# State-space decays kept by head in a hybrid decoder trunk: a scan and broadcast loads in place of matmuls, and the second decay product ahead of the retention

## The chip, the cores and the metric

The kernel runs on one core of a Trainium2 chip. The metric is the device time of one execution in microseconds (us). TensorE (PE) multiplies matrices, VectorE (DVE), ScalarE (ACT) and GpSimd (POOL) work on tiles in the on-chip memory, and SyncE (SP) issues the transfers (DMAs). Each engine has its own list of instructions and works through it in order; where an instruction needs something of another engine or of a DMA, its engine waits there, with all that stands behind it.

## What is computed

Two layers of a decoder trunk on 256 positions of width 1024, all in float32. A layer normalises its input, multiplies it by one wide matrix, feeds three token mixers (a state-space one, retention, and gated linear attention, "gla"), gates and merges their results, and ends with a gated MLP. The change concerns the state-space mixer, and the place of one step of gla. The reference, cut to these:

```python
SEQ, SSM_HEADS, SSM_GROUPS, SSM_STATE = 256, 8, 2, 64
...
def chunked_scalar_decay(q, k, v, log_a, chunk):
    """y_t = sum_{s<=t} (q_t . k_s) exp(sum_{j=s+1..t} log_a_j) v_s per head, chunkwise.
...
xbc = jax.nn.silu(causal_dwconv(xbc, ssm_conv_w, ssm_conv_b))
xs, bm, cm = jnp.split(xbc, [SSM_INNER, SSM_INNER + SSM_GROUPS * SSM_STATE], axis=-1)
...
dt = jax.nn.softplus(dt_raw.astype(jnp.float32) + ssm_dt_bias.astype(jnp.float32))
a = -jnp.exp(ssm_a_log.astype(jnp.float32))
y_ssm = chunked_scalar_decay(ch, bh, xs * dt[..., None].astype(xs.dtype), dt * a, CHUNK)
y_ssm = (y_ssm + ssm_d[:, None] * xs).reshape(bsz, seq, SSM_INNER)
...
alpha_logits = (g_lr @ gla_w_alpha2 + gla_b_alpha).astype(jnp.float32)
log_alpha = (jax.nn.log_sigmoid(alpha_logits) / GLA_GATE_NORMALIZER)
```

So each of the 8 heads has a row `dt` of 256 numbers and a running sum `cum` of `dt * a`, 256 numbers, and the mixer needs, for every pair of positions (s, t) with s <= t, the factor exp(cum_t - cum_s). "The second decay product" is `g_lr @ gla_w_alpha2`.

## The kernel before

**Weights.** All weights come as float32 and are split into a high and a low part, so that three fast matmuls replace one exact one. The unit is a piece of 128x1024 numbers (512 KB). SP loads it (`raw`, L176), ACT casts it to the high part (`whi`, L183), DVE subtracts to get the low part (`wlo`, L184), and PE uses both. Six `whi`, six `wlo` and four `raw` buffers hold pieces ahead of their use. PE's weight matmuls are L227 to L229 (256 columns), L274 to L276 (512 columns) and L1034 to L1036; they write PSUM tiles `mm`. A stream of them ("weight stream") runs through the whole program.

**The rest in between.** `layer` is a generator that yields after each small step of the weight stream. The mixers are generators as well (`ssm`, `ret`, `alpha`, `gla`); `spawn` puts one in a list, and it goes on when as many steps have passed as its last `yield` says. These waits are the table `W`. A scheduler then sets the final order on each engine from what the code says is needed. PE's small matmuls of the mixers write the four PSUM tiles `mx`; a fifth user of `mx` waits until the oldest is read.

**The state-space mixer before** (`ssm`). The projected `dt_raw` lies in `small`: 8 rows with the high part (partitions 0 to 7) and 8 with the low part (64 to 71), 256 positions each. PE multiplies it by a 0/1 matrix `pick` (L572), which adds the two and turns them to positions on partitions: 128x16 (two halves of 8 heads). On that shape come softplus (`log1p`: ACT L297, DVE L298, four times), the product with `a` (L585, tile `da`), and the running sum by three matmuls with a triangle and a matrix of ones (L594 to L596). PE turns the sums back (L609), ACT and DVE split them (L611, L612), and for each pair of heads two matmuls with a column of `pick_r` (L620) spread the rows over 128 partitions; ACT subtracts the partition's own sum (L624, L626), POOL masks (L629) and ACT takes the exponential (L631), which gives a tile `dec` of 128x768 for a pair. There are four pairs and two `dec` buffers, the `st` buffers of retention. Scores of each of the two groups (L637, L638) are multiplied in by DVE (L642), and `scan_out` (L558, 24 small matmuls for a pair) multiplies by the values, four times in a layer. POOL makes the values (L602) and the direct term (L604). L590 turns `xbc` to positions.

**Retention and the decay product before.** `ret` loads its decay tiles (`st`, L720, from `ret_decay`), multiplies in the scores (L729, masked by DVE at L735) and calls `scan_out`. `alpha` does the second decay product (L784: `small` by `wa`, which goes to an `mx` tile), softplus on 128x512, and a scan (L797). It is spawned after the projection `rg`, one projection behind `ret`.

Of the kernel before, what the change touches and what calls it, by code (L numbers as in the profile page):

```python
# [9 lines left out]
F32 = mybir.dt.float32  # L10
# [32 lines left out]
W = (4, 5, 4, 4, 1, 6, 5, 3, 5, 3, 3, 5, 1, 4, 4, 6, 2, 4, 5, 8)  # L43
# [13 lines left out]
for _n, _w in (("mix_g", 8), ("ffn_g", 8), ("conv_w", 24), ("conv_b", 6),  # L57
               ("ssm_g", 4), ("ret_g", 4), ("gla_g", 4), ("b_alpha", 2), ("fconv_w", 132), ("fconv_b", 44),
               ("dt_bias", 8), ("a_log", 8), ("ssm_d", 8)):
    PO[_n] = _at  # L60
    _at += _w
# [66 lines left out]
def hybrid_trunk(ctx: ExitStack, tc: tile.TileContext, xT_in, x_in, wall, par, wa2, cst, phase, dret, fin, gbias, out):  # L128
# [5 lines left out]
    tmp = ctx.enter_context(tc.tile_pool(name="tmp", bufs=4))  # L134
    sm = ctx.enter_context(tc.tile_pool(name="sm", bufs=2))
# [8 lines left out]
    tri = cs[:, CO_TRI:CO_TRI + P]  # L144

    pick_r = cpool.tile([40, 8], F32R, name="pick_r")

    pick = cpool.tile([P, 8], F32, name="pick")
# [143 lines left out]
    def log1p(e, q, p):  # L292

        n = e.shape[-1]
        for i, (_, m) in enumerate(LOG1P):
            qi = q[:, (i % 2) * n:(i % 2 + 1) * n]
            nc.scalar.activation(qi, e, AF.Square, scale=LOG1P_S, bias=lb[:, i:i + 1])  # L297
# [132 lines left out]
    class Mixers:  # L430
# [3 lines left out]
        def __init__(self, l, norm):  # L434
# [5 lines left out]
            self.aneg = sm.tile([P, 8], F32, name="aneg", tag="aneg")  # L440
            nc.scalar.activation(self.aneg, self.pc("a_log", 0, 8), AF.Exp)
# [125 lines left out]
        def ssm(self):  # L567
            xbc, rh, small = self.xbc, self.norm.rh, self.small
            yield W[0]
            pt = mx_tile()  # L570
            for t in range(2):
                nc.tensor.matmul(pt[:, 8 * t:8 * t + 8], lhsT=small[:, t * P:(t + 1) * P], rhs=pick,  # L572
                                 start=(t == 0), stop=(t == 1))
            u, e, dt, da = (sm.tile([P, 16], F32, name=q, tag=q, bufs=1) for q in ("u", "e", "dt", "da"))
            ncum = sm.tile([P, 2, 40], F32, name="nc", tag="nc", bufs=1)
            nc.gpsimd.memset(ncum, 0.0)
            lq = sm.tile([P, 32], F32, name="lq", tag="lq", bufs=1)
            nc.vector.tensor_tensor(u.rearrange("p (t h) -> p t h", t=2), pt[:, :16].rearrange("p (t h) -> p t h", t=2),
                                    self.pc("dt_bias", 0, 8).unsqueeze(1).to_broadcast([P, 2, 8]), ALU.add)
            nc.scalar.activation(e, u, AF.Abs)  # L580
            nc.scalar.activation(e, e, AF.Exp, scale=-1.0)
            log1p(e, lq, dt)
            nc.vector.scalar_tensor_tensor(dt, u, 0.0, dt, ALU.max, ALU.add)
            for t in range(2):
                nc.vector.tensor_tensor(da[:, 8 * t:8 * t + 8], dt[:, 8 * t:8 * t + 8], self.aneg, ALU.mult)  # L585
            xs, val = tok_tile("sg_c"), tok_tile("sg_d")
            for t in range(2):
# [4 lines left out]
                yield W[1]  # L592
# [4 lines left out]
            for o in (0, 32):  # L597
                nc.vector.tensor_scalar(ncum[:, :, o:o + 8], pt[:, 0:16].rearrange("p (t h) -> p t h", t=2), -1.0, None,
                                        ALU.mult)
            for t in range(2):  # L600
                x3 = xs[:, t, :].rearrange("p (h d) -> p h d", h=8)
                nc.gpsimd.tensor_tensor(val[:, t, :].rearrange("p (h d) -> p h d", h=8), x3,  # L602
                                        dt[:, 8 * t:8 * t + 8].unsqueeze(2).to_broadcast([P, 8, 64]), ALU.mult)
# [4 lines left out]
            for t in range(2):  # L608
                nc.tensor.transpose(pt[:40, t * P:(t + 1) * P], ncum[:, t, :], ident)  # L609
# [606 lines left out]
```

## Time and profile before

| what | value |
|---|---|
| median of 3 runs | 924.35 us (923.23, 924.35, 925.10) |
| profiled execution | 925.51 us, span 923.7 us, mean granted clock 0.994 |
| PE busy | 98% of the span |
| DVE, ACT, POOL busy | 77%, 55%, 8% |
| weight pieces of 512 KB | 292, and 10 of half the size |

The span is the part of the execution that the profiler's instructions cover; the 1.8 us beside it are start and end. The profile gives for each group of instructions a line, an engine, an operation and its tiles, with busy time; "idle before" is the time for which the engine stood still just ahead of them, and the arrow names what ended that. PE's matmuls overlap one another: the start of one to the start of the next is what one costs, not its own length. A weight matmul of 512 columns costs 0.23 us this way.

### The profile page before, as it was taken

The page shows a single profiled execution, that of the slowest core. Times are in us where ns is not written, and L with a number is a line of the kernel's source. Part 1 is how long each engine was busy: PE and PEld are TensorE (multiplying, and loading weights), DVE is VectorE, ACT ScalarE, POOL GpSimd, SP SyncE. Part 2 cuts the span into 40 slices and gives each one's busy share as a digit, 9 for nine tenths or more (in the row PEclk, how much of TensorE's full clock was granted, in tenths as well). Part 3 has the DMA queues.
Part 4 walks back from the last instruction along what each step waited for, and adds up shares of the span by engine and source line. Part 5 has one row for each costly group of instructions (what it writes and reads, how often), then busy time and mean ns, then how long its engine had stood idle before and what let it go on. Part 6 is the DMA issues. An engine that isn't in the chain of part 4 may idle for free.

```text
span 923.7 us, 15389 instructions
## 1 busy us (share of the span) xinstructions
PE 903.4 (98%) x5918; PEld 803.0 (87%) x5918; DVE 710.5 (77%) x1111; ACT 505.3 (55%) x748; POOL 78.4 (8%) x74
## 2 busy tenths in 40 slices
PE   8999999999999999999999999999999999999995
PEld 7879878888889999999898897888888999999994
DVE  6976879576768878778799578877757797777775
ACT  6665445454456555555566644544445575555542
POOL 3032200003200000000002131000210000000001
PEclk9999999999999999999999999999999999999998
DMA  7774654556565665555465656455666565555531
GB/s 248 272 255 154 221 193 157 172 179 212 183 194 162 190 190 193 184 184 184 148 187 181 202 173 214 161 156 159 209 200 202 161 202 183 184 186 189 187 102 45
DMA packets 51289, 169.95 MB, mean 184 GB/s; under 512 B 5968, under 2 KB 8336, under 8 KB 51088
## 3 DMA queue, kind: packets, MB, share of 16 engines
q1 hardware_dynamic: 50928, 168.46, 56.6%
q8 instruction: 46, 0.75, 0.3%
q10 hardware_dynamic: 288, 0.52, 0.1%
q14 instruction: 27, 0.22, 0.1%
HBM read 165.81 MB, written 1.05 MB: 181 GB/s over the span
## 4 chain that ended last, share of the span: by engine, by line
PE 85%; DVE 6%; DMA 3%; issue 3%; ACT 1%; SPq 1%; POOL 0%; ACTq 0%; DVEq 0%; POOLq 0%
PE mm L227 12%; PE mm L228 12%; PE mm L229 11%; PE mm L274 11%; PE mm L276 11%; PE mm L275 11%; PE mx L1034 4%; PE mx L1035 4%; PE mx L1036 4%; DVE wlo L184 2%; DMA raw<-w_all 1%; DMA st<-ret_decay 1%; PE mx L542 1%; SPq L704 1%; DMA x_t<-x_t 1%
## 5 line engine op out<-in xcount | busy, mean ns | idle before, releaser
L184 DVE TENSOR_TENSOR wlo<-raw,whi 128x1024 fp32r<-128x1024 f32 (+1 forms) x300 | 376.2, 1257 | 124.8 <-ACT whi L183 121.6
L183 ACT CAST whi<-raw 128x1024 fp32r<-128x1024 f32 (+1 forms) x302 | 311.5, 1034 | 279.4 <-PE mm L276 112.7
L227 PE MATMUL mm<-slot_h,whi 128*128 128x256 f32 x992 | 282.3, 285 | 2.4 <-ACT slot_h L302 2.4
L228 PE MATMUL mm<-slot_l,whi 128*128 128x256 f32 x992 | 281.5, 284 | 0.1
L229 PE MATMUL mm<-slot_h,wlo 128*128 128x256 f32 x992 | 281.5, 284 | 0.0
L274 PE MATMUL mm<-whi,slot_h 128*128 128x512 f32 x512 | 203.7, 398 | 0.0
L275 PE MATMUL mm<-wlo,slot_h 128*128 128x512 f32 x512 | 200.6, 392 | 0.0
L276 PE MATMUL mm<-whi,slot_l 128*128 128x512 f32 x512 | 200.5, 392 | 0.0
L227 PEld LDWEIGHTS mm<-slot_h,whi 128*128 128x128 f32 x992 | 190.5, 192 | 5.4 <-ACT slot_h L302 2.8
L228 PEld LDWEIGHTS mm<-slot_l,whi 128*128 128x128 f32 x992 | 190.7, 192 | 2.1 <-DVE slot_l L303 0.3
L229 PEld LDWEIGHTS mm<-slot_h,wlo 128*128 128x128 f32 x992 | 190.7, 192 | 0.1
L274 PEld LDWEIGHTS mm<-whi,slot_h 128*128 128x128 f32 x512 | 96.2, 188 | 21.1 <-issue 0.7
L276 PEld LDWEIGHTS mm<-whi,slot_l 128*128 128x128 f32 x512 | 96.1, 188 | 20.1
L275 PEld LDWEIGHTS mm<-wlo,slot_h 128*128 128x128 f32 x512 | 96.3, 188 | 18.5
L1024 DVE SCALAR_TENSOR_TENSOR tm<-tm,par 128x255 f32<-128x255 f32 (+1 forms) x176 | 73.6, 480 | 0.7 <-ACT tm L1022 0.7
L1034 PE MATMUL mx<-whi,slot_h 128*128 128x512 f32 x176 | 69.1, 392 | 0.0
L1035 PE MATMUL mx<-wlo,slot_h 128*128 128x512 f32 x176 | 69.0, 392 | 0.0
L1036 PE MATMUL mx<-whi,slot_l 128*128 128x512 f32 x176 | 68.5, 389 | 0.0
L1022 ACT ACTIVATE tm<-tm,par 128x256 f32<-128x256 f32 x88 | 48.0, 592 | 4.3 <-DVE tm L1017 4.3
L1017 DVE TENSOR_TENSOR tm<-mm,r_bc 128x512 f32<-128x512 f32 x44 | 30.4, 691 | 23.0 <-PE mm L229 23.0
L1028 ACT CAST slot_h<-tm 128x256 fp32r<-128x256 f32 x44 | 17.8, 405 | 49.1 <-DVE tm L1027 49.1
L1036 PEld LDWEIGHTS mx<-whi,slot_l 128*128 128x128 f32 x176 | 33.1, 188 | 7.1
(187 smaller groups left out, 716.7 us busy)
## 6 DMA issues: line engine op xcount, KB each, us to landing
raw<-w_all SPq DMA_DIRECT2D x292, 512.0 KB, 3.6
gate_b<-gate_b SPq DMA_DIRECT2D x12, 256.0 KB, 3.3
st<-ret_decay SPq DMA_DIRECT2D x8, 384.0 KB, 4.4
raw<-w_all SPq DMA_DIRECT2D x10, 256.0 KB, 3.9
x_t<-x_t SPq DMA_DIRECT2D x4, 256.0 KB, 5.9
xt<-x_tok SPq DMA_DIRECT2D x1, 1024.0 KB, 8.0
r_c<-q SPq DMA_DIRECT2D x16, 64.0 KB, 2.0
r_d<-q SPq DMA_DIRECT2D x16, 64.0 KB, 2.1
```

Of the source, the lines that this page charges most:

```text
L183: nc.scalar.copy(h_out, r_in)
L184: nc.vector.tensor_tensor(l_out, r_in, h_out.bitcast(F32), ALU.subtract)
L227: nc.tensor.matmul(o, lhsT=wh[:, c], rhs=ah[:, k, :], start=first, stop=False)
L228: nc.tensor.matmul(o, lhsT=wh[:, c], rhs=al[:, k, :], start=False, stop=False)
L229: nc.tensor.matmul(o, lhsT=wl[:, c], rhs=ah[:, k, :], start=False, stop=last)
L274: nc.tensor.matmul(acc[t], lhsT=ah[:, k, c], rhs=wh, start=first, stop=False)
L275: nc.tensor.matmul(acc[t], lhsT=ah[:, k, c], rhs=wl, start=False, stop=False)
L276: nc.tensor.matmul(acc[t], lhsT=al[:, k, c], rhs=wh, start=False, stop=last)
L1024: nc.vector.scalar_tensor_tensor(a[:, d:], u[:, :T - d], mx.pc("fconv_w", 3 * ct + 2 - d), a[:, d:], ALU.mult, ALU.add)
L1034: nc.tensor.matmul(o, lhsT=ah[:, a, tok], rhs=wh, start=first, stop=False)
L1035: nc.tensor.matmul(o, lhsT=ah[:, a, tok], rhs=wl, start=False, stop=False)
L1036: nc.tensor.matmul(o, lhsT=al[:, a, tok], rhs=wh, start=False, stop=last)
```

## The change

- The 8 heads stay on partitions. DVE adds the two parts of `small` (8x256, L570 in the changed kernel), softplus runs on 8x256 (ACT L293, DVE L294), a DVE scan makes `cum` (L577). `dt` and `cum` lie in one tile of 40 partitions. `dt_bias` and `a_log` become one number for each of 8 partitions.
- `cum` is written to memory (L581), and for each pair of heads two loads copy its rows to all 128 partitions (L587: whole rows of 1024 bytes; L588: their second halves of 512 bytes): 384 KB for a pair, four pairs in a layer. Nothing of that is done by PE or by ACT's copies any more.
- Two small transposes (L602) give `dt` and minus `cum` by position (DVE copies L605, L606). The exponential takes minus `cum` as its bias: four instructions for a pair (L618, L619) in place of four subtracting copies and one exponential.
- Scores of both groups are computed at once (L627), and `scan_out` is called for two pairs at a time (L554).
- The table `W` has other numbers, and one fewer.
- `alpha` is spawned before `ret`, a projection earlier.

```diff
-W = (4, 5, 4, 4, 1, 6, 5, 3, 5, 3, 3, 5, 1, 4, 4, 6, 2, 4, 5, 8)
+W = (7, 2, 3, 6, 7, 1, 4, 6, 5, 3, 5, 1, 4, 4, 7, 2, 4, 5, 8)
...
             xbc, rh, small = self.xbc, self.norm.rh, self.small
+
+            bias, (ue, lq, rows) = self.pc("dt_bias")[:8], (t_mix() for _ in range(3))
+            rows = rows[:40, :T]
+            nc.gpsimd.memset(rows, 0.0)
+            u, e, q, dt, cum = ue[:8, :T], ue[:8, T:], lq[:8], rows[:8], rows[32:40]
+            nc.vector.tensor_tensor(u, small[:8], small[64:72], ALU.add)
+            nc.scalar.activation(e, u, AF.Abs, bias=bias)
+            nc.scalar.activation(e, e, AF.Exp, scale=-1.0)
+            log1p(e, q, dt)
+            nc.vector.tensor_scalar(u, u, bias, 0.0, ALU.add, ALU.max)
+            nc.vector.tensor_tensor(dt, dt, u, ALU.add)
+            nc.vector.tensor_scalar(u, dt, self.aneg, None, ALU.mult)
+            nc.vector.tensor_tensor_scan(cum, ones[:8], u, 0.0, ALU.mult, ALU.add)
+
             yield W[0]
-            pt = mx_tile()
-            for t in range(2):
-                nc.tensor.matmul(pt[:, 8 * t:8 * t + 8], lhsT=small[:, t * P:(t + 1) * P], rhs=pick,
-                                 start=(t == 0), stop=(t == 1))
...
+            there = dram.tile([8, T], F32, name="cum", tag="cum")
+            nc.sync.dma_start(there, cum)
+
+            def spread(h2):
+
+                dec = mix.tile([P, 2, 384], F32, name="dec", tag="st", bufs=2)
+                two_rows = there[2 * h2:2 * h2 + 2, :]
+                nc.sync.dma_start(dec[:, :, 0:256], two_rows.partition_broadcast(P))
+                nc.sync.dma_start(dec[:, :, 256:384], two_rows[:, P:].partition_broadcast(P))
+                return dec
+
+            yield W[1]
+            d0, d1 = spread(0), spread(1)
+            yield W[2]
...
-            nc.tensor.matmul(pt[:, 0:8], lhsT=tri, rhs=da[:, 0:8], start=True, stop=False)
-            nc.tensor.matmul(pt[:, 8:16], lhsT=ones[:, :P], rhs=da[:, 0:8], start=False, stop=False)
-            nc.tensor.matmul(pt[:, 8:16], lhsT=tri, rhs=da[:, 8:16], start=False, stop=True)
...
+            for t in range(2):
+                nc.tensor.transpose(pt[:, 40 * t:40 * t + 40], rows[:, t * P:(t + 1) * P], ident[:40, :40])
...
-                for j in range(2):
-                    h = 2 * h2 + j
-                    nc.tensor.matmul(pb[:, j * T:(j + 1) * T], lhsT=pick_r[:, h:h + 1].to_broadcast([40, P]), rhs=cum,
-                                     start=(j == 0), stop=(j == 1))
...
+                for j in range(2):
+                    h = 2 * h2 + j
+                    nc.scalar.activation(dec[:, j, 0:256], dec[:, j, 0:256], AF.Exp, bias=ncum[:, 0, h:h + 1])
+                    nc.scalar.activation(dec[:, j, 256:384], dec[:, j, 256:384], AF.Exp, bias=ncum[:, 1, h:h + 1])
...
+            yield W[3]
+            sc = scores()
+            for d in (d0, d1):
+                masked(d, sc[0])
             yield W[4]
...
             self.scan_out(py, 0, d0, val)
+            self.scan_out(py, 1, d1, val)
+            yield W[5]
+            d2, d3 = spread(2), spread(3)
             yield W[6]
+            for h2, d in ((2, d2), (3, d3)):
+                decay(h2, d)
+                masked(d, sc[1])
             yield W[7]
...
         finish(ssm)
-        ret = spawn(mx.ret(), 1)
+        spawn(mx.alpha())
+        ret = spawn(mx.ret(), 2)
         acc = yield from tok_major(l, "rg", x_act)
         mx.wr = mx.take_silu(acc, "r_a")
         yield
-        spawn(mx.alpha())
         yield from branches(0, gts)
```

Three places in the final order of instructions. The first is DVE's list at the start of the state-space mixer in layer 0, before (L466 and L471 are the convolution, L475 writes `small`, L184 makes the low part of a weight piece; numbers behind a name tell tiles apart):

```order
L475 TENSOR_TENSOR small_475<-mm_452,r_bc_331 128x256 [waits PE_49]
L459 TENSOR_TENSOR tm_439<-mm_378,r_bc_331 128x512
L471 SCALAR_TENSOR_TENSOR xbc_333<-tm_375,xbc_333 128x512 [waits Activation_49]
L184 TENSOR_TENSOR wlo_481<-raw_479,whi_480 128x1024 [waits DMAHW2_49]
L466 SCALAR_TENSOR_TENSOR xbc_333<-tm_439,half_159,xbc_333 128x255 [waits Activation_49] x2
L466 SCALAR_TENSOR_TENSOR xbc_333<-tm_439,half_159,xbc_333 128x254 [waits DVE_49] x2
L466 SCALAR_TENSOR_TENSOR xbc_333<-tm_439,half_159,xbc_333 128x253 [waits DVE_49] x2
L184 TENSOR_TENSOR wlo_499<-raw_497,whi_498 128x1024 [waits DMAHW4_49,PE_49]
```

and in the changed kernel, where L462, L467 and L180 are the old L466, L471 and L184:

```order
L471 TENSOR_TENSOR small_473<-mm_450,r_bc_329 128x256 [waits PE_49]
L455 TENSOR_TENSOR tm_437<-mm_376,r_bc_329 128x512
L467 SCALAR_TENSOR_TENSOR xbc_331<-tm_373,xbc_331 128x512 [waits Activation_49]
L570 TENSOR_TENSOR tx_475<-small_473 8x256 [waits DVE_49]
L462 SCALAR_TENSOR_TENSOR xbc_331<-tm_437,half_159,xbc_331 128x255 [waits DVE_49,Activation_49]
L462 SCALAR_TENSOR_TENSOR xbc_331<-tm_437,half_159,xbc_331 128x255 [waits Activation_49]
L462 SCALAR_TENSOR_TENSOR xbc_331<-tm_437,half_159,xbc_331 128x254 [waits DVE_49] x2
L462 SCALAR_TENSOR_TENSOR xbc_331<-tm_437,half_159,xbc_331 128x253 [waits DVE_49] x2
L574 TENSOR_SCALAR tx_475<-tx_475,par0_76 8x256 [waits Activation_49]
L294 SCALAR_TENSOR_TENSOR tx_477<-tx_476,tx_475 8x256 [waits Activation_49]
L180 TENSOR_TENSOR wlo_498<-raw_496,whi_497 128x1024 [waits DMAHW2_49]
```

The low part of that weight piece stood behind the convolution's L471; now it stands behind L570, six L462, L574 and the first L294, two of which wait for ACT.

The second place is SP's list in layer 0, before (the weight pieces that are loaded during the state-space mixer):

```order
L176 DMA raw_664<-w_all 128x1024 [waits DMAHW3_49,DMAHW7_49,DVE_49,Activation_49]
L176 DMA raw_692<-w_all 128x1024 [waits DMAHW0_49,DVE_49,Activation_49]
L176 DMA raw_715<-w_all 128x1024 [waits DMAHW1_49,DMAHW5_49,DVE_49,Activation_49]
L176 DMA raw_733<-w_all 128x1024 [waits DMAHW2_49,DVE_49]
L176 DMA raw_766<-w_all 128x1024 [waits DMAHW3_49,DVE_49]
L494 DMA gate_b_688<-gate_b 128x512 [waits DVE_49]
```

and in the changed kernel (L172 is the old L176):

```order
L172 DMA raw_686<-w_all 128x1024 [waits DMAHW3_49,DMAHW7_49,DVE_49,Activation_49]
L581 DMA cum_562<-tx_477 8x256 [waits DVE_49,Pool_49]
L172 DMA raw_714<-w_all 128x1024 [waits DMAHW5_49,DMAHW0_49,DVE_49]
L587 DMA dec_593<-cum_562 128x2x256 [waits DMAHW4_49]
L588 DMA dec_593<-cum_562 128x2x128
L587 DMA dec_596<-cum_562 128x2x256 [waits Pool_49]
L588 DMA dec_596<-cum_562 128x2x128 [waits DMAHW1_49]
L172 DMA raw_740<-w_all 128x1024 [waits DMAHW2_49,DVE_49]
L490 DMA gate_b_710<-gate_b 128x512 [waits DMAHW3_49,DVE_49]
L172 DMA raw_758<-w_all 128x1024 [waits Activation_49]
```

The write of `cum` and the first four broadcast loads now stand between weight loads; the four loads of the second pairs stand seven weight loads further down.

The third place is PE's list around the second decay product in layer 0, before, where it stands behind retention's second scores:

```order
L729 MATMUL mx_1450<-r_c_964,r_d_1149 128x256 [waits PE_49]
L729 MATMUL mx_1451<-r_c_964,r_d_1149 128x256 [waits PE_49]
L729 MATMUL mx_1450<-r_c_964,r_d_1149 128x128
L729 MATMUL mx_1451<-r_c_964,r_d_1149 128x128
L274 MATMUL mm_1410<-whi_1284,slot_h1_89 128x512 [waits Activation_49]
L275 MATMUL mm_1410<-wlo_1285,slot_h1_89 128x512
L276 MATMUL mm_1410<-whi_1284,slot_l1_90 128x512
L274 MATMUL mm_1411<-whi_1284,slot_h1_89 128x512
L275 MATMUL mm_1411<-wlo_1285,slot_h1_89 128x512
L276 MATMUL mm_1411<-whi_1284,slot_l1_90 128x512
L274 MATMUL mm_1410<-whi_1312,slot_h1_89 128x512
L784 MATMUL mx_1457<-small_475,wa_164 128x256 [waits DVE_49]
```

and in the changed kernel, where 24 weight matmuls lie between it and retention's first scores (L722):

```order
L272 MATMUL mm_1292<-whi_1144,slot_l0_88 128x512
L777 MATMUL mx_1307<-small_473,wa_164 128x256 [waits DMAHW3_49]
L777 MATMUL mx_1307<-small_473,wa_164 128x256
L270 MATMUL mm_1291<-whi_1144,slot_h0_87 128x512
...
L722 MATMUL mx_1368<-r_c_979,r_d_1173 128x256 [waits DMAHW4_49,DMAHW7_49,DMAHW3_49,DMAHW0_49]
L722 MATMUL mx_1369<-r_c_979,r_d_1173 128x256 [waits DMAHW1_49,DMAHW5_49,DVE_49,PE_49]
L722 MATMUL mx_1368<-r_c_979,r_d_1173 128x128
L722 MATMUL mx_1369<-r_c_979,r_d_1173 128x128
```

The product no longer waits for DVE, and it now comes before all of retention's scores.

## Rows read from the trace of the kernel before

**Rows 1.** The page: busy time; the chain that ended last; the costliest ACT group.

```profile
PE 903.4 (98%) x5918; PEld 803.0 (87%) x5918; DVE 710.5 (77%) x1111; ACT 505.3 (55%) x748; POOL 78.4 (8%) x74
...
PE 85%; DVE 6%; DMA 3%; issue 3%; ACT 1%; SPq 1%; POOL 0%; ACTq 0%; DVEq 0%; POOLq 0%
...
L183 ACT CAST whi<-raw 128x1024 fp32r<-128x1024 f32 (+1 forms) x302 | 311.5, 1034 | 279.4 <-PE mm L276 112.7
```

**Rows 2.** Waits of PE: line, what it waited for, us in total, times, longest us.

```profile
PE mx L784 <- DVE st L735: 2.3, 2, 1.7
...
PE mx L594 <- DVE da L585: 1.2, 1, 1.2
```

**Rows 3.** The chain of waits: start us, us, engine, tile, line, count.

```profile
66.03 0.63 PE mx L637 x2
...
134.86 0.85 PE mx L729 x8
...
487.74 0.34 PE mx L572 x4
```

**Rows 4.** Timeline of PE, layer 0: start us, us, line, tiles, [idle before].

```profile
55.78 0.39 PE L594 MATMUL mx<-da,cs 128*128 128x8 f32 x2 [1.19 <-DVE da L585]
...
56.48 0.48 PE L276 MATMUL mm<-whi,slot_l 128*128 128x512 f32 x1
...
58.18 0.38 PE L609 MATMUL mx<-cs,nc 128*40 128x128 f32 x2
58.31 0.48 PE L274 MATMUL mm<-whi,slot_h 128*128 128x512 f32 x1
...
63.64 0.39 PE L276 MATMUL mm<-whi,slot_l 128*128 128x512 f32 x1
63.96 0.50 PE L620 MATMUL mx<-slot_h,pick_r 40*128 40x256 f32 x2
64.39 0.50 PE L274 MATMUL mm<-whi,slot_h 128*128 128x512 f32 x1
64.72 0.40 PE L275 MATMUL mm<-wlo,slot_h 128*128 128x512 f32 x1
```

**Rows 5.** Timelines of PE (layer 1) and DVE (layer 0) at the second decay product.

```profile
580.19 1.13 PE L784 MATMUL mx<-small,wa 128*128 128x256 f32 x4 [1.71 <-DVE st L735]
...
127.86 1.02 DVE L735 TENSOR_TENSOR st<-st,mx 128x384 f32<-128x384 f32 x2 [2.60 <-DMA st<-ret_decay]
```

**Rows 6.** Timelines of DVE, ACT and PE at the mixer's start, layer 0.

```profile
40.10 1.22 DVE L184 TENSOR_TENSOR wlo<-raw,whi 128x1024 fp32r<-128x1024 f32 x1
41.23 2.45 DVE L466 SCALAR_TENSOR_TENSOR xbc<-tm,half,xbc 128x255 f32<-128x255 f32 x6
...
41.63 1.05 ACT L183 CAST whi<-raw 128x1024 fp32r<-128x1024 f32 x1 [1.19 <-DMA raw<-w_all]
...
44.73 0.40 PE L275 MATMUL mm<-wlo,slot_h 128*128 128x512 f32 x1
```

**Rows 7.** Timelines of ACT and PE ahead of the running sum, layer 1.

```profile
500.09 1.05 ACT L183 CAST whi<-raw 128x1024 fp32r<-128x1024 f32 x1 [0.88 <-PE mm L276]
...
502.62 0.28 PE L594 MATMUL mx<-da,cs 128*128 128x8 f32 x2
```

**Rows 8.** Groups by line and shape: tiles, count, busy us, mean ns of one, idle before.

```profile
L642 DVE TENSOR_TENSOR dec<-dec,mx 128x768 f32<-128x768 f32 x8 | 7.6, 949 | 3.4 <-ACT dec L631 3.4
...
L602 POOL TENSOR_TENSOR sg_d<-sg_c,dt 128x512 f32<-128x512 f32 x4 | 6.0, 1514 | 280.7 <-ACT whi L183 246.5 <-DVE dt L583 34.1
...
L797 DVE TENSOR_TENSOR_SCAN gla_work<-cs,gla_work 128x256 f32<-128x256 f32 x4 | 2.5, 678 | 0.0
...
L612 DVE SCALAR_TENSOR_TENSOR slot_h<-mx,slot_h 8x256 fp32r<-8x256 f32 x2 | 0.8, 417 | 0.2 <-ACT slot_h L611 0.2
```

**Rows 9.** DMA issues: tiles, queue, count, KB each, median us from issue to landing.

```profile
st<-ret_decay SPq DMA_DIRECT2D x8, 384.0 KB, 4.4
...
r_c<-q SPq DMA_DIRECT2D x16, 64.0 KB, 2.0
```

More of the change, by code (lines that the diff above doesn't have):

```diff
@@ L58 @@
                ("ssm_g", 4), ("ret_g", 4), ("gla_g", 4), ("b_alpha", 2), ("fconv_w", 132), ("fconv_b", 44),
-               ("dt_bias", 8), ("a_log", 8), ("ssm_d", 8)):
+               ("dt_bias", 1), ("a_log", 1), ("ssm_d", 8)):
     PO[_n] = _at
@@ L577, in ssm @@
[L577 to L583, printed above, removed]
@@ L630, in decay, with scores @@
                                             compare_op=ALU.is_ge, fill=NEG, base=0, channel_multiplier=-1)
-                nc.scalar.activation(dec, dec, AF.Exp)
-                return dec
-            def score(g):
-                c = slice(64 * g, 64 * g + 64)
-                pt = mx_tile()
-                nc.tensor.matmul(pt[:, 0:256], lhsT=xbc[c, 4, 0:P], rhs=xbc[c, 5, :], start=True, stop=False)
-                nc.tensor.matmul(pt[:, 256:384], lhsT=xbc[c, 4, P:T], rhs=xbc[c, 5, P:T], start=False, stop=True)
+                for j in range(2):
+                    h = 2 * h2 + j
+                    nc.scalar.activation(dec[:, j, 0:256], dec[:, j, 0:256], AF.Exp, bias=ncum[:, 0, h:h + 1])
+                    nc.scalar.activation(dec[:, j, 256:384], dec[:, j, 256:384], AF.Exp, bias=ncum[:, 1, h:h + 1])
+            def scores():
+                pt = [mx_tile() for _ in range(2)]
+                for o, w, k in ((0, 256, 0), (256, 128, P)):
+                    for g in range(2):
+                        c = slice(64 * g, 64 * g + 64)
+                        nc.tensor.matmul(pt[g][:, o:o + w], lhsT=xbc[c, 4, k:k + P], rhs=xbc[c, 5, k:], start=(k == 0),
+                                         stop=(k > 0))
                 return pt
@@ L817, in gla @@
             nc.gpsimd.memset(sg, 0.0)
-            yield W[16]
+            yield W[15]
             pt = [mx_tile() for _ in range(2)]
@@ L1079, in rest_ahead @@
             nc.vector.tensor_copy(gmask, cs[:, CO_GM:CO_GM + P])
-            for o, p, n in ((pick_r, 32, 40), (pick, 64, P)):
-                nc.vector.tensor_tensor(o, ident[:n, :8], ident[:n, p:p + 8], ALU.add)
             for j in range(4):
@@ L1164, in _lay_params @@
         put(l, "fconv_b", cols(i["ffn_conv_b"][l]))
-        for name, key in (("dt_bias", "ssm_dt_bias"), ("a_log", "ssm_a_log"), ("ssm_d", "ssm_d")):
-            put(l, name, np.broadcast_to(i[key][l].reshape(1, 8), (P, 8)))
+        put(l, "dt_bias", i["ssm_dt_bias"][l].reshape(8, 1))
+        put(l, "a_log", i["ssm_a_log"][l].reshape(8, 1))
+        put(l, "ssm_d", np.broadcast_to(i["ssm_d"][l].reshape(1, 8), (P, 8)))
     return par
```

86 lines of the change are left out of this document (27 added, 59 removed).

## The prediction, made before the changed kernel was run

> **What bounds the kernel now.** The page comes first: PE is busy for 98% of the span and makes up 85% of the chain that ended last [rows 1]. The kernel ends when PE has worked through its list, so an edit is worth what it takes from that list or from PE's waits, and work on other engines costs nothing unless PE comes to wait for it. The second look is at what PE waits for. Two of its waits concern this change: the second decay product L784 waits 2.3 us for retention's masks L735, twice, and the running sum L594 waits 1.2 us for the state-space decays, once [rows 2]. The third look is at the weights. ACT's cast of a weight piece stands idle mostly because PE has not yet given a buffer back (112.7 us of its idle time behind L276) [rows 1]: the pieces lie ahead of PE, and PE saved time is not given back to them. The exception is the start of layer 0, where the cast at 41.63 waits for a DMA [rows 6].
>
> Prices on PE's list are read from start to start. A weight matmul of 512 columns takes 0.23 us. A change from weight matmuls to small ones costs about 0.1 us going and 0.1 coming: 63.64 to 63.96 is 0.32, and 64.39 to 64.72 is 0.33 [rows 4]. I count 0.2 for an insertion.
>
> **The change part by part.** *Matmuls removed*, per layer: `pick` 0.34 us [rows 3]; the running sum 0.70 (55.78 to 56.48); the transposes back 0.13 (58.18 to 58.31); four spreads by `pick_r` at 0.43 (63.96 to 64.39), 1.72 [rows 4]. Together 2.89. The scores were two sets at 0.63, 1.26; now both are computed together by four matmuls in two row halves, the form and size of retention's scores, which take 0.85 [rows 3]; that leaves 0.41. The two new small transposes cost 0.13, like those removed. In the order the mixer's insertions fall from 12 to 6 in a layer: 6 x 0.2 = 1.2. Sum: 2.89 + 0.41 - 0.13 + 1.2 = 4.4, for two layers **8.8 us** off PE's list. The bounds are 3.4 a layer (scores without gain, an insertion at 0.1) and 4.6.
>
> *Waits removed*: L594 is gone with its 1.2. L784 waited because its `mx` tile was held by retention's scores, which DVE could not read before `st` had landed: DVE stood 2.60 us for that DMA, PE 1.71 at the longest [rows 5]. Now the product stands 24 weight matmuls ahead of retention's first scores, behind nothing that waits for a DMA; its operands are long there. All 2.3 go. What is late next on that path is the second half of retention's scores, which need the same `st`; they come 7 us later than L784 did (134.86 [rows 3]) and don't wait now. Sum **3.5 us**; lower bound 2.5, if the alpha softplus on DVE now delays retention's first masks.
>
> *DVE and ACT at the start, layer 0.* DVE was doing a weight piece's low part at 40.10, done at 41.3, and PE used it at 44.73 [rows 6]. In the new order it stands behind L570, the six convolution steps, L574 and the first L294. From 40.10: an 8x256 instruction takes 0.42 [rows 8], the six take 2.45 [rows 6], which is 42.97; L574 0.42; the first L294 needs ACT's squares, and ACT does the cast of 41.63 (to 42.68), an exponential and a square first, some 0.4 each, to about 43.5; L294 to 43.9; the piece itself 1.22 [rows 6] to 45.15. PE comes 0.9 us earlier than before, at 43.85, since `pick` and one separate transpose insertion are no longer ahead. **Wait 1.3 us**, bounds 0 and 2.5 (the same again, if ACT's part is one cast later).
>
> *DVE ahead of the transposes* L602. They need the scan, so softplus must be over; its four steps cost 0.42 on DVE instead of 0.17. In layer 1 the order puts three weight pieces between its last steps, and the cast of one of these waits for PE itself (500.09, 0.88 us [rows 7]): 501.14 for the cast, 1.22 for the low part, about 0.6 for the scan (0.68 by a scan of 128x256 [rows 8]), 502.9. PE stood at L594, the corresponding place, at 502.62 [rows 7], and comes about 0.9 earlier. **Wait 1.2**, bounds 0 and 1.5. In layer 0 scan and PE meet at about 52.9: 0.3, bounds 0 and 1.
>
> *The broadcast loads.* Nothing in the trace copies one row to 128 partitions. The low bound is 4.4 us for a pair, a load of 384 KB in rows of 3 KB; the high bound is 12, if they move like six of the 64 KB loads in 1 KB rows, at 2.0 each, one behind the other [rows 9]. I take 4.4 to 6: the row of the same size, with some room for shorter rows. The Trainium skill ("DMA: Bandwidth & Descriptors", Specifications) wants runs of at least 512 B for line rate; these runs have 512 and 1024 B, so by that page the low bound would hold, and no run here shows it for a broadcast.
>
> In layer 0: scan over at 52.9; `cum` lands 2.0 us later, like the 64 KB transfer [rows 9], or a little more, 55 to 55.5; loads issued by 57.5, landed at 60 to 63. POOL is busy with values and direct term, four products at 1.51 [rows 8], from 56 to 62, and only then masks; the exponentials of two pairs (ACT, 1.7 each) and the DVE products (0.95 each [rows 8]) end at 65.8 and 67.4. PE reaches `scan_out`, 88 weight matmuls behind 45.15 with 1.75 of insertions, at 67.2, and needs the second pair 0.8 later. So the margin is near zero: 0 to 2 us of wait, I take **0.3**. The loads of the second pairs leave when PE has read the first, and PE is back 66 weight matmuls (15 us) later: 6 for the loads, some 6 for masks and exponentials, margin 3. In layer 1 the weight matmuls between are more, margin 7. The SP queue: behind the wait for `cum` to land and behind the loads of the second pairs, weight loads are queued for 3 to 5 us; pieces that lie ahead cover it.
>
> *Small things.* `dt_bias` and `a_log` shrink, `pick` is not built: nothing on PE's list.
>
> The sum: -8.8 - 3.5 + 1.3 + 1.2 + 0.3 + 0.3 = -9.2. Against the profiled execution, 925.51, that is 916.3. The median of the runs is 924.35, 1.16 below it; the same sum from there gives **915.1 us**. With every bound of these terms on the good side (-9.2 - 3.5) it is 911.6; on the bad side (-6.8 - 2.5 + 2.5 + 1.5 + 1 + 2) 922.1, though hardly all together.
>
> **The rivals.** (1) *Layer 0's start eats the gain there.* The pieces loaded at 32 to 50 us are thin; if the by-head chain delays not one piece but the next two as well (each stands behind one more L294 that waits for ACT), 1.3 becomes about 5 us: 919. For: the cast waits for DMA there, so DVE has no slack to catch up. Against: DVE's list is no longer than before by more than 2 us in all.
>
> (2) *Loads a little late.* Call the time from issue to the landing of two pairs L. The first `scan_out` in layer 0 waits for L - 6, the second for L - 9, in layer 1 the first for L - 13 and the second for L - 9. At 8 to 10 us these are 2 to 6 us in all: 917 to 921. For: the margin in layer 0 is near zero. Against: POOL's products hide the landing until 62.
>
> (3) *Slower: the broadcast loads are the bound.* At 12 us a pair, one after another, L is 24, and the four waits are 18, 15, 11 and 15, together 59, less the 9.5 gained elsewhere: about 973. It decides from L = 6; the time of before is passed at L = 11, where the waits are 5, 2, 0 and 2. For: all loads of a layer read the same eight rows, in short runs. Against: loads of 384 KB land in 4.4 us beside the weights [rows 9].
>
> (4) *The second decay product just moves its wait.* PE would wait as long at retention's scores instead, since `alpha`'s softplus now stands on DVE where the masks do: 917.5. Against: those scores have no wait in the trace now.
>
> **How the numbers follow.** Forecast 0.64 (own range 911.5 to 918); (1) 0.13, (2) 0.09, (4) 0.05, (3) 0.09. To hold 8 in 10 the range begins at the forecast's lower end and takes in (1), (4) and most of (2): **911 to 920**. About 0.2%, 1.85 us, is what a measurement can tell here. Faster by more: all but (3) and the far end of (1) and (2), 0.87; within it 0.04; slower 0.09.
>
> **What would show it.** Right: L784's successor L777 has no wait row on PE; L594 to L596 and L620 are gone, and PE's busy time falls by about 9 us; the broadcast loads land within 6 us and `scan_out` waits less than 1 us. A wait of PE for `wlo` around 44 us shows the layer 0 step, a wait of L602 for DVE the scan. Wrong: landing times beyond 8 us; a PE wait at L554 for `dec` of several us; a wait of L722 for the masks; or PE's busy time unchanged.

## The result

The changed kernel is slower. Its median is 932.44 us (930.01 to 933.68) against 924.48 for the kernel before on the same chip; the ratio of the runs is 1.0067, with a 95% interval of 1.0048 to 1.0087. The prediction was 915.1, range 911 to 920, with 0.09 for slower. Its profiled execution took 933.46 us, 7.95 more than that of before.

The page of the changed kernel, busy time and the chain that ended last:

```profile
PE 899.6 (97%) x5882; PEld 802.4 (86%) x5882; DVE 713.8 (77%) x1109; ACT 502.2 (54%) x738; POOL 78.1 (8%) x74
...
PE 85%; DVE 7%; DMA 3%; ACT 2%; issue 2%; SPq 1%; POOL 0%; DVEq 0%; ACTq 0%
```

PE's busy time fell by 3.8 us [rows 1], not by the 9 that were forecast. What PE waited for, whole program (line, what for, us in total, times, longest):

```profile
PE mx L538 <- DVE tx L559: 16.4, 2, 9.2
PE mm L223 <- ACT slot_h L298: 2.3, 1, 2.3
PE mx L1068 <- POOL ones L146: 1.1, 1, 1.1
PE mx L602 <- DVE tx L577: 0.5, 1, 0.5
```

The waits of L784 and L594 [rows 2] are gone, as forecast. A new one stands in their place, twice 7 to 9 us: L538, the transposes by which the finished state-space output goes to the branch product, waits for L559, the last step of its normalisation on DVE. In the kernel before the same transposes (L542) waited 0.35 us in layer 0. The timeline of PE in layer 0:

```profile
97.92 0.39 PE L271 MATMUL mm<-wlo,slot_h 128*128 128x512 f32 x1
107.53 0.69 PE L538 MATMUL mx<-cs,tx 128*128 128x128 f32 x2 [9.23 <-DVE tx L559]
...
111.01 0.63 PE L270 MATMUL mm<-whi,slot_h 128*128 128x512 f32 x1
111.44 0.63 PE L271 MATMUL mm<-wlo,slot_h 128*128 128x512 f32 x1
...
113.70 0.40 PE L271 MATMUL mm<-wlo,slot_h 128*128 128x512 f32 x1
113.94 0.40 PE L272 MATMUL mm<-whi,slot_l 128*128 128x512 f32 x1
```

The wait costs a second time. Behind it weight matmuls start 0.43 us apart until about 113, then 0.23 again: PE's clock is at the lower of its two levels, 1.2 GHz, after PE stood still. The windows show the granted clock (the first of the last three columns) at 0.67 in the 8 us behind the wait:

```profile
98.00:108.00 10.00, 0.77 (x5) 0.47 (x3) 9.47 (x21) 2.79 (x3) 3.46 (x2) 0.76 0.63 189
108.00:116.00 8.00, 8.00 (x29) 6.52 (x28) 4.29 (x7) 3.79 (x7) 0.00 (x0) 0.67 0.61 241
```

The same table shows who worked in the 10 us in which PE stood: DVE, for 9.47 of them. DVE was behind. The sum of PE's listed waits rose by 11.6 us (8.7 before, 20.3 now), PE's busy time, the slow matmuls included, fell by 3.8; the difference, 7.8, is what the change cost.

### The profile page after: what moved, and what is told of

The parts are those of the page before. It is cut to its first block, busy times and chain, and to the rows that moved or that the text cites. A ratio compares the mean times of both kernels' runs of the same rounds, so it can differ in the third digit from the quotient of the medians.

```text
span 931.7 us, 15353 instructions
## 1 busy us (share of the span) xinstructions
PE 899.6 (97%) x5882; PEld 802.4 (86%) x5882; DVE 713.8 (77%) x1109; ACT 502.2 (54%) x738; POOL 78.1 (8%) x74
## 4 chain that ended last, share of the span: by engine, by line
PE 85%; DVE 7%; DMA 3%; ACT 2%; issue 2%; SPq 1%; POOL 0%; DVEq 0%; ACTq 0%
PE mm L223 11%; PE mm L224 11%; PE mm L225 11%; PE mm L270 11%; PE mm L272 11%; PE mm L271 11%; PE mx L1027 4%; PE mx L1028 4%; PE mx L1029 4%; DVE wlo L180 2%; DMA raw<-w_all 1%; PE mx L554 1%; PE mx L538 1%; DMA dec<-cum 1%; DVE xbc L462 1%
## 5 line engine op out<-in xcount | busy, mean ns | idle before, releaser
L180 DVE TENSOR_TENSOR wlo<-raw,whi 128x1024 fp32r<-128x1024 f32 (+1 forms) x300 | 373.2, 1247 | 116.0 <-ACT whi L179 112.3
```

The source lines that it names most:

```text
L180: nc.vector.tensor_tensor(l_out, r_in, h_out.bitcast(F32), ALU.subtract)
```

## Where DVE lost its time

The timeline of DVE in layer 0, from the products of the second pairs' decays with their scores (L632) to the end of the normalisation. L180 are weight pieces, L691 and L692 rotary products of retention, L661 the first step of the normalisation:

```profile
79.52 1.23 DVE L180 TENSOR_TENSOR wlo<-raw,whi 128x1024 fp32r<-128x1024 f32 x1 [4.42 <-ACT whi L179]
80.66 0.95 DVE L632 TENSOR_TENSOR dec<-dec,mx 128x768 f32<-128x768 f32 x1
83.20 0.95 DVE L632 TENSOR_TENSOR dec<-dec,mx 128x768 f32<-128x768 f32 x1 [1.59 <-issue]
...
87.02 3.58 DVE L180 TENSOR_TENSOR wlo<-raw,whi 128x1024 fp32r<-128x1024 f32 x2
92.04 0.69 DVE L691 TENSOR_TENSOR q<-mm,r_a 128x512 f32<-128x512 f32 x1 [1.44 <-DMA r_c<-q]
92.65 1.22 DVE L180 TENSOR_TENSOR wlo<-raw,whi 128x1024 fp32r<-128x1024 f32 x1
93.78 0.68 DVE L661 TENSOR_TENSOR tx<-mx,sg_c 128x512 f32<-128x512 f32 x1
...
106.79 1.29 DVE L559 TENSOR_TENSOR tx<-tx,rs_y 128x512 f32<-128x512 f32 x2
```

Two things are to be seen. First, DVE stood idle for 4.42 us for a cast by ACT and 1.59 us ahead of the second product. Second, the last `scan_out`, which started at 84.14, ended at 85.7, and the normalisation that needs nothing else began at 93.78, behind pieces and rotary products. The idle 4.42 us come from further up. Timelines of ACT, POOL, SP (its rows are DMAs issued) and PE:

```profile
77.22 0.91 ACT L618 ACTIVATE dec<-dec,nc 128x256 f32<-128x256 f32 x2 [3.98 <-POOL dec L614]
...
83.02 4.06 ACT L179 CAST whi<-raw 128x1024 fp32r<-128x1024 f32 x4
...
76.78 0.41 POOL L614 TENSOR_SCALAR_AFFINE_SELECT dec<-dec 128x256 f32<-128x256 f32 x1 [12.79 <-DMA dec<-cum]
...
81.57 0.41 POOL L614 TENSOR_SCALAR_AFFINE_SELECT dec<-dec 128x256 f32<-128x256 f32 x1 [0.56 <-DMA dec<-cum]
...
58.96 12.38 SPq L172 DMA_DIRECT2D raw<-w_all  x6
71.43 0.39 SPq L587 DMA_DIRECT2D dec<-cum  x1
...
66.57 1.62 PE L554 MATMUL mx<-sg_d,dec 128*64 128x64 f32 x48
```

The loads of the third and fourth pair leave at 71.43 and later. The first `scan_out` calls (L554) had given their tiles back at 68.2; the other 3 us went by in SP's list, where six weight loads stand ahead, the last of which waited until DVE had freed a `raw` buffer. The first load lands at 76.8, the last at 81.6. POOL's masks (L614) wait for them, ACT's exponentials wait for POOL, and ACT works in order: the casts behind the exponentials come late, one at 78.45 and a burst of four at 83.02. DVE has no pieces to do while ACT waits, and too many afterwards. PE doesn't feel it at once, since its weights lie ahead; it feels it 20 us later, at L538.

ACT's order is not the whole of it. Two weight pieces that SP issued right behind the broadcast loads, at 73.45 and 74.53, took 9.3 and 9.5 us to land (3.5 is the median of the program), so ACT could not have cast these two before 82.8 and 84.0, held or not. The late loads hold DVE in two ways, through ACT and through the pieces that share the queues with them; the experiments below move the loads and so both at once, and what each is worth is not shown.

For comparison the kernel before, timelines of PE and DVE: the normalisation (L668) begins with the last `scan_out`, and the transposes stand just behind its end.

```profile
98.78 0.92 PE L558 MATMUL mx<-sg_d,dec 128*64 128x64 f32 x24
...
99.28 0.69 DVE L668 TENSOR_TENSOR tx<-mx,sg_c 128x512 f32<-128x512 f32 x1
...
109.27 1.29 DVE L563 TENSOR_TENSOR tx<-tx,rs_y 128x512 f32<-128x512 f32 x2
...
110.02 0.44 PE L542 MATMUL mx<-cs,tx 128*128 128x128 f32 x2 [0.35 <-DVE tx L563]
```

In layer 0 DVE reached the end of the normalisation at 110.6 before and at 108.1 after: it gained 2.5 us. PE reached the transposes at 109.7 before and at 98.3 after: it gained 11.4, by the matmuls and waits that it was spared and by the new numbers of `W`, which put L538 26 weight matmuls (6 us) further forward in its list.

## The experiments

Theory A: PE is simply too early for a normalisation that stands late in DVE's list. Theory C: the late loads of the second pairs hold ACT, its casts and so DVE. Rivals: B, the DMA wait of 1.44 us in front of L691; D, a chain that hangs on PE's own progress; F, DVE full whatever the order; and the moved decay product. All ratios are to runs of the kernel before on the same chip, with 95% intervals; the medians come from several chips, so kernels are compared by their ratios. The last column has all waits at that line; it also serves retention's branch, which is noted where it waits.

| kernel | median us | ratio | PE at L538, us |
|---|---|---|---|
| the change | 932.44 | 1.0067 [1.0048, 1.0087] | 16.4 |
| e1, L538 later | 926.43 | 0.9999 [0.9983, 1.0015] | 6.5 |
| e2, and last scan_out earlier | 924.90 | 0.9994 [0.9979, 1.0010] | below 0.2 |
| e3, third buffer for q | 929.33 | 1.0034 [1.0016, 1.0052] | 10.9 |
| e4, all loads together | 920.93 | 0.9945 [0.9925, 0.9965] | 5.4 |
| e5, decay product back | 935.34 | 1.0093 [1.0070, 1.0117] | 16.5 (1.0 of it retention's) |
| e6, before, decay product ahead | 926.52 | 1.0006 [0.9992, 1.0021] | 0.7 (L542) |
| e7, e4 with scan_out early | 916.23 | 0.9885 [0.9860, 0.9911] | none |
| e8, second loads twice | 935.59 | 1.0097 [1.0076, 1.0118] | 15.8 |
| e9, e7 with decay product back | 917.13 | 0.9915 [0.9893, 0.9937] | 1.0 (retention's) |
| e10, e7 with late loads | 929.08 | 1.0037 [1.0023, 1.0050] | none |
| e11, e7 with later retention | 917.04 | 0.9903 [0.9877, 0.9929] | 1.6 |

### Moving PE's transposes

```diff
-W = (7, 2, 3, 6, 7, 1, 4, 6, 5, 3, 5, 1, 4, 4, 7, 2, 4, 5, 8)
+W = (7, 2, 3, 6, 7, 1, 4, 6, 15, 3, 5, 1, 4, 4, 7, 2, 4, 5, 8)
```

> The changed kernel with one number of the table W: the wait ahead of the state-space branch's last transposes L538 is 15 steps instead of 5. In PE's list they then stand 72 instead of 53 weight matmuls behind the last scan_out, 4.3 us later; DVE's list stays as it is up to there. Theory A (PE comes too early for a normalisation chain on DVE that stands late in DVE's list, and the 16.4 us of PE waiting for L559 are the loss): the two waits 9.2 and 7.1 fall by 4.3 each, to about 8 together, the clock of PE stays high for longer, 920 to 924 us. Rival D (DVE's chain hangs on PE's own progress, through buffers that PE gives back): the chain moves along and the wait stays near 16; 932.

The wait fell by 9.9 us, from 16.4 to 6.5, a little more than the 8.6 by which the transposes were moved. D falls: DVE's chain does not move along with PE. Two waits of PE in e1:

```profile
PE mx L538 <- DVE tx L559: 6.5, 4, 3.8
PE mm L271 <- DVE wlo L180: 1.7, 1, 1.7
```

The time, 926.43, was above the 920 to 924 expected; by the ratio, on the chip of the change, it would be 924.4. Part of that is the second row: a wait of 1.74 us at 45.02, the start of layer 0, which the changed kernel's own profile doesn't show.

```diff
-W = (7, 2, 3, 6, 7, 1, 4, 6, 5, 3, 5, 1, 4, 4, 7, 2, 4, 5, 8)
+W = (7, 2, 3, 6, 7, 1, 4, 4, 15, 3, 5, 1, 4, 4, 7, 2, 4, 5, 8)
```

> As the run before it, and the last two scan_out calls wait 4 steps instead of 6: they move 12 weight matmuls forward on PE, and on DVE the first instruction of the normalisation (L661) stands ahead of the rotary product that waits for the r_c loads. Between last scan_out and L538 now lie 84 weight matmuls, 19 us. Theory A: PE's wait for L559 is gone or below 1 us, PE's clock stays at 1.00, time 910 to 915, which is what the prediction said of the change without this wait. Rival D: wait above 8 us, 925 or more. If a new wait at L554 for dec appears, it shows the price of the loads of the second pairs.

Half a miss. The wait at L538 is gone, as A and not D says, but the time is that of e1, not 910 to 915. The waits went on down the program. Of e2:

```profile
PE mx L722 <- DVE gla_work L783: 2.7, 2, 1.4
...
PE mx L554 <- DVE dec L632: 1.2, 1, 1.2
```

The transposes now stand directly ahead of the second decay product, their consumers on DVE come together with its softplus, and retention's scores L722 wait for the `mx` tile; L554, moved forward, meets the late loads. Behind the waits of L722 the granted clock was 0.86 from 116 to 128 us. Moving instructions in PE's list brought the time back to that of the kernel before, but not to the forecast: a part of the wait moves on, as long as DVE is behind.

### The DMA wait ahead of the rotary product

```diff
-                q = tmp.tile([P, 512], F32, name="q", tag="q", bufs=2)
+                q = tmp.tile([P, 512], F32, name="q", tag="q", bufs=3)
```

> The changed kernel with three buffers for the rotary product q instead of two, so that L691 for the second projection no longer waits for the r_c loads; otherwise the same places on every engine. Theory A: DVE's waits of 1.4 and 2.1 us go, the chain comes that much earlier, the waits at L538 fall to about 7.5 and 5: 927 to 930. Rival B (that DMA wait is the cause): the waits at L538 fall below 2, 912 to 917.

The wait fell by 5.5 us to 10.9, somewhat more than A says (12.5) for 1.4 and 2.1 us of DMA wait; in layer 0 PE also came 1.2 us later than in the change, after 1.7 us of wait at its start. B, which wanted the wait below 2, falls. A part of the lateness, not its cause.

### The loads of the second pairs

```diff
+                if h2 < 2:
+                    dec = mix.tile([P, 2, 384], F32, name="dec", tag="st", bufs=2)
+                else:
+                    far = mix.tile([P, D], F32, name="far", tag=("m_lo", "m_hi")[h2 - 2])
+                    dec = far[:, :768].rearrange("p (j c) -> p j c", j=2)
...
-            d0, d1 = spread(0), spread(1)
+            d0, d1, d2, d3 = (spread(h2) for h2 in range(4))
...
-            d2, d3 = spread(2), spread(3)
```

> The changed kernel with tiles of their own (the space of the two merge tiles) for the decays of the third and fourth pair, loaded together with the first two, so that no load waits for scan_out and ACT is not held by exponentials that wait for a load. L661 keeps its place in DVE's list behind the same weight pieces; one rotary product less ahead of it. Theory C (ACT is held for 4 to 6 us by the loads of the second pairs, its casts come late, DVE falls behind and starts the normalisation late): L661 starts some 5 us earlier, the waits at L538 fall to about 3 each, 919 to 924. Theory A without C (only the place in the list): the waits stay at 7 to 9, 929 to 933.

The late loads are what costs most: 5.4 us of wait and 920.93, inside the 919 to 924 of theory C. Timelines of DVE and PE in e4, where L636 is the last product with the scores and L664 the start of the normalisation:

```profile
68.80 0.95 DVE L636 TENSOR_TENSOR far<-far,mx 128x768 f32<-128x768 f32 x1 [0.43 <-ACT far L623]
...
88.52 0.68 DVE L664 TENSOR_TENSOR tx<-mx,sg_c 128x512 f32<-128x512 f32 x1
...
103.05 0.69 PE L538 MATMUL mx<-cs,tx 128*128 128x128 f32 x2 [3.67 <-DVE tx L559]
```

The last product is done at 69.8 instead of 84.1, and the normalisation begins at 88.5 instead of 93.8, 5.3 us earlier, with `scan_out` at its old place. Not all of the 5.3 is theory C: in e4 a rotary product (L691 in the change, 0.69 us and 1.44 of DMA wait) stands behind the start of the normalisation instead of ahead of it. The end of the normalisation is the fairer measure, 103.6 instead of 108.1.

The opposite test issues the suspected loads twice.

```diff
-                nc.sync.dma_start(dec[:, :, 0:256], two_rows.partition_broadcast(P))
-                nc.sync.dma_start(dec[:, :, 256:384], two_rows[:, P:].partition_broadcast(P))
+                for _ in range(2 if h2 > 1 else 1):
+                    nc.sync.dma_start(dec[:, :, 0:256], two_rows.partition_broadcast(P))
+                    nc.sync.dma_start(dec[:, :, 256:384], two_rows[:, P:].partition_broadcast(P))
```

> The changed kernel with the broadcast loads of the third and fourth pair issued twice, one behind the other, which doubles their landing time from 6 to about 11 us and changes nothing else. Theory C (ACT, held by exponentials that wait for these loads, holds the casts, and so DVE): scan_out L554 waits 3 to 5 us and the normalisation starts that much later, so L538 still waits about 8; 938 to 944. Theory A without C: what is waited at L554 is no longer waited at L538, 931 to 935.

Waits of PE in e8:

```profile
PE mx L538 <- DVE tx L559: 15.8, 2, 8.4
PE mx L554 <- DVE dec L633: 1.8, 2, 1.2
```

By the ratios it cost 0.3%, with intervals that overlap; C expected 6 to 12 us more than the change, A at most 3. The wait at L538 stayed, while 1.8 us came at L554. The edit did less than its expectation says: the last load of the second pairs landed at 84.5 instead of 81.6, and the normalisation began at 94.2, 0.4 us later than in the change, since it stands one rotary product further forward. So this run doesn't tell the two apart.

e10 does it better. It is the changed kernel with the numbers of `W` of e7 (below), and its code differs from e7 only in the place and the tiles of these loads; in the final order its last `scan_out` calls stand 1 to 2 us further back.

```diff
-W = (7, 2, 3, 6, 7, 1, 4, 6, 5, 3, 5, 1, 4, 4, 7, 2, 4, 5, 8)
+W = (7, 2, 3, 6, 7, 1, 1, 1, 13, 3, 5, 1, 4, 4, 7, 2, 4, 5, 8)
```

> The changed kernel with the same numbers of W as e7_early_scan, but the loads of the second pairs still behind the first scan_out calls: only the place of the loads tells it from e7_early_scan. Theory C (the loads of the second pairs are what comes late): PE now waits for them at the last scan_out calls, 6 to 9 us in each layer, 926 to 935. If the numbers of W were the whole cause: as e7_early_scan, 914 to 918.

Waits and timeline of PE in e10:

```profile
PE mx L554 <- DVE dec L632: 9.5, 3, 4.7
...
79.32 1.55 PE L554 MATMUL mx<-sg_d,dec 128*64 128x64 f32 x24 [4.63 <-DVE dec L632]
```

929.08 against 916.23 for e7, 1.5% between the two ratios: that is what the late loads cost with these numbers of `W`. With those of the change it is 1.2% (the change against e4). The other way round, the numbers of `W` are worth 0.3% with late loads (the change against e10) and 0.6% with early ones (e4 against e7). Wherever `scan_out` is put, the second pairs' late loads have to be paid, at L554 directly or at L538 by way of DVE.

### With both mended

```diff
-W = (7, 2, 3, 6, 7, 1, 4, 6, 5, 3, 5, 1, 4, 4, 7, 2, 4, 5, 8)
+W = (7, 2, 3, 6, 7, 1, 1, 1, 13, 3, 5, 1, 4, 4, 7, 2, 4, 5, 8)
```

(with the loads as in e4)

> The kernel with all broadcast loads issued together, and with the waits of W at the second pairs cut to 1 step each and 13 steps ahead of L538. The last scan_out calls stand 48 weight matmuls further forward on PE, the normalisation's first instruction comes ahead of six rotary products on DVE, and L538 stands 78 weight matmuls behind the last scan_out. Theory C with A: PE waits at neither place, PE's clock stays high, 911 to 916, the time that the prediction gave to the change. Rival F (DVE has no time left in this stretch, whatever the order): the wait comes back at retention's scores or at the gla products, 918 to 923.

916.23 us, 1.15% (0.89 to 1.40) below the kernel before and 1.8% below the change. On its chip that is 9.3 us below the kernel before, and the forecast for the change was 9.2 below. That the totals agree is in part luck: e7 has an order and tiles that the sum didn't price, and PE's busy time fell by 5.8 us instead of 8.8. Timelines of PE and DVE in e7:

```profile
72.60 1.62 PE L554 MATMUL mx<-sg_d,far 128*64 128x64 f32 x48
...
79.04 0.68 DVE L664 TENSOR_TENSOR tx<-mx,sg_c 128x512 f32<-128x512 f32 x1
...
91.72 1.29 DVE L559 TENSOR_TENSOR tx<-tx,rs_y 128x512 f32<-128x512 f32 x2
92.92 0.70 PE L538 MATMUL mx<-cs,tx 128*128 128x128 f32 x4
...
131.13 0.89 PE L725 MATMUL mx<-r_c,r_d 64*128 64x256 f32 x6 [1.05 <-DVE st L731]
```

The normalisation takes as long as in the change (79.04 to 93.0), but it begins 14.7 us earlier than in the change, and PE arrives as it ends. So F falls for the normalisation: DVE has the time, if it isn't held, though with nothing in hand. One wait is left in the stretch, retention's scores for a mask that waits for its decay tile.

e11 puts these scores later; its edit against e7:

```diff
-W = (7, 2, 3, 6, 7, 1, 1, 1, 13, 3, 5, 1, 4, 4, 7, 2, 4, 5, 8)
+W = (7, 2, 3, 6, 7, 1, 1, 1, 13, 3, 5, 1, 6, 3, 7, 2, 4, 5, 8)
```

> The kernel e7_early_scan with retention's last scores two steps later (12 weight matmuls, 2.7 us) and its last scan_out one step less behind them, since the one wait left in the stretch was PE at these scores for a mask that waited for its decay tile, 1.1 us, with a slower clock behind it. If that wait is what is left of the loss in layer 0: 2 to 3 us less than e7_early_scan, 912 to 914. If DVE has no time left there: the same wait at the next place, 915 to 917.

A miss: that wait went, but 1.6 us came at L538 in layer 0, ahead of the scores that were moved, and the ratio is that of e7 within the intervals. The time is what was expected if DVE has none left there.

### The second decay product

```diff
+        ret = spawn(mx.ret(), 1)
         acc = yield from tok_major(l, "rg", x_act)
         mx.wr = mx.take_silu(acc, "r_a")
         yield
+        spawn(mx.alpha())
```

(in place of the two calls ahead of `rg`; in e5 on the changed kernel, in e9 on e7. e6 is the opposite edit on the kernel before.)

> The changed kernel with the second decay product put back behind the projection rg and retention spawned with a wait of 1: only the state-space part of the change is left. Theory C: L538 stands at the same place and its waits stay near 16 us together; the wait of L784's successor for retention's masks may come back with up to 2.3 us. 930 to 936. If the moved decay product were the loss (its softplus taking DVE from the normalisation), the waits at L538 would fall by 5 or more: 922 to 927.

> The kernel before with the second decay product ahead of retention, and nothing else. The prediction's price: its wait of 2.3 us goes, 922 to 923. Rival F (DVE is busy for 97% of the 18 us ahead of it in the kernel before, so softplus there delays the normalisation or the masks): as much is waited at L542 or at retention's scores, 924 to 927.

> The kernel e7_early_scan, in which PE doesn't wait at the normalisation, with the second decay product put back behind the projection rg and retention spawned with 1: this prices the second part of the change where nothing else hides it. Prediction's step: the product waits for retention's masks again, 2.3 us and a slower clock behind them: 918 to 921. Rival (the wait only changes its place, as it did in e6_alpha_only): within 1 us of e7_early_scan.

In e5 the state-space waits at L538 are still 15.5 us: the moved product is not the loss. In e6, where it is the only edit, nothing is gained. Waits of PE in e6 and, with the product back, in e9:

```profile
PE mx L729 <- DVE st L735: 2.1, 3, 1.5
...
PE mx L780 <- DVE st L731: 1.9, 2, 1.0
```

In e6 L784 no longer waits, and retention's scores L729 wait 2.1 us for the same masks, which still wait for `st`. In e9 L780, the product at its old place, waits 1.9 us. With the state-space part of the change, the kernels with the product moved forward are ahead: the change by 0.0026 against e5, e7 by 0.0030 against e9, that is 2.4 and 2.8 us, but in each pair the intervals overlap (e9: 0.9893 to 0.9937 against 0.9860 to 0.9911). So in the kernel before the move gains nothing; whether it gains its 2.3 us beside the rest of the change these runs can't tell.

## The prediction, step by step

**Matmuls off PE's list: right, or a little too much.** PE came to the first `scan_out` at 66.57 (predicted 67.2), without a wait. In e7, where nothing hides it, retention's first scores start at 111.28, in the kernel before at 115.10, though 6 weight matmuls (1.4 us) and the decay product (0.7) have been moved ahead of them: 5.9 us in layer 0, for which the steps gave 4.4 + 1.2 less small waits. PE's busy time in whole programs without the wait at the normalisation is 5.8 us (e7) and 7.4 us (e9) below that of before; the step said 8.8.

**Waits at the start and at L602: right in kind, too large here.** L602 waited 0.5 us once (1.5 predicted for two layers). The wait for `wlo` near 44 us isn't in the changed kernel's profile, but it is in e1 with 1.74 us: 1.3 was predicted.

**The broadcast loads: one pair was near, two together and the consequence wrong.** Issue to landing, median us of one load:

```profile
dec<-cum SPq DMA_DIRECT2D x8, 256.0 KB, 5.9
...
dec<-cum SPq DMA_DIRECT2D x8, 128.0 KB, 6.5
```

A pair (384 KB) takes some 6 us, the top of what I took (4.4 to 6, with a far bound of 12 [rows 9]); rival (3) is out. But two pairs issued together share the queues: from the first issue to the last landing it was 9.2 us for the first two pairs of layer 0 and 10.1 for the second two, and single loads took up to 8.6, where I had named 8 as a sign of being wrong. That is the condition of rival (2), 8 to 10 us, yet none of the waits that it computed came. I cited the Trainium skill ("DMA: Bandwidth & Descriptors", Specifications) for runs of 512 bytes being enough for line rate. No run here shows these loads alone. From 71.4 to 81.6 us the DMA engines moved 251 GB/s (186 on average), and weight pieces of 512 KB issued beside the broadcast loads took 7.2 us (median of four) instead of 3.5: the loads shared busy queues, and whether short runs or common source rows cost anything besides can't be told. The loads of the second pairs also didn't leave "when PE has read the first", but 3 us later, behind weight loads in SP's list. `scan_out` didn't wait for the decays of the second pairs, which were done at 84.15, when PE arrived at 84.14; I had a margin of 3.

**The step that failed** is a term that the sum doesn't have: it puts the stretch behind the last `scan_out` at nothing. All that PE was spared was counted as gain, and the late loads were held only against PE: "margin 3", "pieces that lie ahead cover it". They cover PE. I asked of each wait whether PE's weights would run out, and not what the waiting engine would have done meanwhile. ACT, held by exponentials, makes DVE idle for 4.4 us and then late, weight pieces land late beside the loads, and DVE has a chain besides the weights, the normalisation, for which nothing lies ahead. The profile of before showed that this chain ended when PE came (PE's waits; two of the four, 0.35 and 0.34 us, are the state-space transposes, the others retention's):

```profile
PE mx L542 <- DVE tx L563: 1.7, 4, 0.5
```

On this path without slack the 11.4 us by which PE came earlier, against 2.5 for DVE, became 9.2 us of wait in layer 0, and 7.1 in layer 1: 16.4 us where the sum had 0, and the lower clock behind each is paid on top.

**The order as a term.** I read the new numbers of `W` as part of the code motion and priced what was moved past what. That they put L538 6 us further forward on PE was in the order, and I didn't hold it against the DVE chain that it waits for. With the loads early, an order that starts the normalisation sooner and leaves 78 instead of 53 weight matmuls between the last `scan_out` and L538 is worth another 0.6% (e7 against e4).

**The second decay product: rival (4) right in e6, open in the change.** In the changed kernel neither L777 nor retention's scores L722 wait, as forecast, but PE comes to both late, from L538. The 2.3 us at L784 did move to retention's scores when this was the only edit (e6). I argued that "those scores have no wait in the trace now"; e6 shows that they had none because L784 took it first. Rival (4) had 0.05. Beside the rest of the change the price stays open, as the overlap of e5 and e9 with their partners says.

**Rivals and chances.** None of them had the mechanism that decided. (2) and (3) had its first half, the late loads, but looked for the wait at `scan_out`. (1), the start of layer 0, had no wait in the changed kernel's profile, and at most 1.7 us in the other runs.

## What to carry to other kernels

When work is taken off the engine that sets the pace, look up each place where it meets another engine's chain and how much that chain has in hand: a wait of a few tenths there (0.35 us at L542) means none, and the gain ends at that place. A wait that an in-order engine takes on itself, for a load say, delays everything that it would have done next and everybody who lives on that; buffers that cover one consumer don't cover the others. Loads that depend on nothing that changes late should be issued together and early, with tiles of their own: here that turned a loss of 0.7% into a gain of 0.55%, and with their consumers moved forward into one of 1.15%.

## What was unexpected of the hardware

The length of a wait doesn't tell what it costs in clock. After 9.23 us at L538 in the changed kernel weight matmuls stood 0.43 us apart for 5 us. In e7 the granted clock was 1.00 from 110 to 131 us, and behind the wait of 1.05 us at 131.13 they stood 0.43 apart as well:

```profile
133.39 0.63 PE L270 MATMUL mm<-whi,slot_h 128*128 128x512 f32 x1
133.82 0.63 PE L271 MATMUL mm<-wlo,slot_h 128*128 128x512 f32 x1
```

That wait lay between two of retention's scores, small matmuls all around; the granted clock from 131 to 139 us was 0.79. Longer waits had no such effect: behind 1.19 us at L594 [rows 4] and 1.71 us at L784 in layer 1 [rows 5] in the kernel before, and 1.74 us at 45.02 in e1, the granted clock stayed at 1.00 (55.7 to 62, 580 to 592 and 45 to 52 us). What decides between these cases no run here shows. So a wait that is short in the list of waits can cost more than its length, and need not.
